# Score blocks on four 32-column tiles of TensorE, and one product with w per chunk in a delta-rule scan

## The chip, the cores and the metric

The kernel runs on one core of a Trainium2 chip. A core has five engines with an instruction stream each: TensorE (PE; its weight loads, PEld, are shown apart), VectorE (DVE), ScalarE (ACT), GpSimd (POOL) and SyncE (SP, which issues DMAs). The metric is the time of one execution on the device, in microseconds (us); less is better.

## The reference, cut to what matters

The program computes two blocks of a network on 1024 tokens of width 1024. The first block holds a mixer with four gated heads and one with twelve. The second holds a hybrid mixer, one branch of which is a delta-rule scan (gdn), on the latent tokens (1024) and before that on a context of 256 tokens. The two pieces that the change touches are these.

```
def _chunk_gated_scan(q, k, v, log_g):        # CHUNK = 32 keys; both directions are needed
    ...
    s = jnp.einsum('bnthk,bnshk->bnhts', q * jnp.exp(b - ref), k * jnp.exp(ref - b))
    s = jnp.where(np.tril(np.ones((CHUNK, CHUNK), bool)), s, 0.0)
    o_intra = jnp.einsum('bnhts,bnshv->bnthv', s, v)
    ...

def gdn_chunked(q, k, v, g, beta, s0):        # chunks of 64 tokens
    ...
    u = jnp.einsum('bnhij,bnhjv->bnhiv', tm, vc * bc[..., None])
    w = jnp.einsum('bnhij,bnhjk->bnhik', tm, kb * jnp.exp(gc)[..., None])
    attn = jnp.einsum('bnhik,bnhjk->bnhij', qc, kc) * decay
    qg = qc * jnp.exp(gc)[..., None]
    kend = kc * jnp.exp(gc[..., -1:] - gc)[..., None]
    def step(s, inp):
        v_new = u_i - jnp.einsum('bhlk,bhkv->bhlv', w_i, s)
        o_i = jnp.einsum('bhlk,bhkv->bhlv', qg_i, s) + jnp.einsum('bhij,bhjv->bhiv', a_i, v_new)
        s = s * ge_i[..., None, None] + jnp.einsum('bhlk,bhlv->bhkv', ke_i, v_new)
        return s, o_i
```

The kernel does not step through `v_new`: for every chunk it forms the products of w with `kend` (here `ke`) and with `attn` (here the "row" or `at`), so that a step of the scan is one small matrix product with the state.

## The kernel before, in words

**Order of the program.** Nobody writes out the order of the instructions: the framework (`schedule_with_timeline_sim=True`) orders each engine's stream when the kernel is built, by the data each instruction needs, by the buffers of the tile pools and by priorities (`g.up()` raises one). On the chip each engine then takes its stream in that order.

**Gated heads (`Gated.unit`).** A head has 128 key features on the partitions and 1024 tokens. It is cut into units of n = 256 tokens, for each of two directions d; so there are (4 + 12) heads x 4 x 2 = 128 units. In a unit, VectorE and ScalarE make scaled copies of q and k: `u_qt`/`u_kt` (scaled within 32 tokens), `u_qa`/`u_kb` (across neighbouring groups of 32), `u_qh`/`u_kh` (across halves of 64). GpSimd makes `u_qh` (L239) and `u_qd` (L241). Then come the score products, for each of the ng = 2 blocks of 128 tokens, all in fp32 with K = 128: one 128x128 product of `u_kt` and `u_qt` (L247), and over parts of its result two 32x32 products of `u_kb` and `u_qa` (L249, L250, or L253, L254) and one 64x64 product of `u_kh` and `u_qh` (L251 or L255). The result goes from PSUM to `A` by ScalarE (d = 1) or by a masked copy on VectorE (d = 0, L261). Each fp32 product appears in the trace as two records of LDWEIGHTS and MATMUL. Between the score products the scheduler puts the projections of the next heads (L139 to L141), the state updates `o<-V,u_kdT` (L225), the transposes `a<-ident,u_kd` (L214) and the outputs (L276 to L280). The first four heads run with the adaLN table in the background (L957 to L975), the twelve others with the context path of the second block.

**The scan (`gdn_scan`).** On the latent tokens it runs for three pairs of heads, and `prepare` for two directions of each: six times in all. `hTb` and `hwb` are wide buffers that hold one direction. In `prepare`, `huw` is made on GpSimd and VectorE and multiplied with `hTb` (L1607); this gives u (in `huw`) and w (in `hwb`). GpSimd makes `ke` (L1616) and the base of `A` (L1619). Then TensorE makes for eight chunk pairs and two heads w times `ke` (L1624, 128 stationary columns and 64 moving) and `ke` times u (L1632, 64x64), which give `A` and `B`. After these, a row of decays comes by DMA, passes ScalarE, VectorE, two `affine_select` on GpSimd (L1651), ScalarE, and is multiplied with `kq` on GpSimd (L1654); TensorE then makes w times this row (L1658, 64 moving) and the row times u (L1667, 64x64), which give `Q` and `O`. `carry` is the chain over 16 chunks (L1696, L1698). On the context (`fin` is given) only `A` and `B` are made. During the first latent pairs another branch (ssd, L1250 to L1346) runs beside the scan. Behind the scan comes the output projection (`MixersOut.group`), whose weights pass through the buffers `mraw`.

Of the kernel before, what the change touches and what calls it, by code (L numbers as in the profile page):

```python
# [10 lines left out]
F32 = mybir.dt.float32  # L11
# [143 lines left out]
class Gated:  # L155
# [14 lines left out]
    def unit(self, d, u, q, k, lg):  # L170
# [71 lines left out]

        ap = g.psum("a")
        for i in range(ng):
            o = i * P
            w = lambda a, lo, hi: a[:, o + lo:o + hi]
            nc.tensor.matmul(ap[:, o:o + P], w(kt, 0, P), w(qt, 0, P), start=True, stop=True)  # L247
            if d == 0:
                nc.tensor.matmul(ap[0:32, o + 32:o + 64], w(kb, 0, 32), w(qa, 32, 64), start=True, stop=True)  # L249
                nc.tensor.matmul(ap[64:96, o + 96:o + 128], w(kb, 64, 96), w(qa, 96, 128), start=True, stop=True)  # L250
                nc.tensor.matmul(ap[0:64, o + 64:o + 128], w(kh, 0, 64), w(qh, 64, 128), start=True, stop=True)  # L251
            else:
                nc.tensor.matmul(ap[32:64, o:o + 32], w(kb, 32, 64), w(qa, 0, 32), start=True, stop=True)  # L253
                nc.tensor.matmul(ap[96:128, o + 64:o + 96], w(kb, 96, 128), w(qa, 64, 96), start=True, stop=True)  # L254
                nc.tensor.matmul(ap[64:128, o:o + 64], w(kh, 64, 128), w(qh, 0, 64), start=True, stop=True)  # L255
# [1272 lines left out]
def gdn_scan(g, pool, wide, n, fm_out, rows, inv, hp, s0, fin=None):  # L1528
# [53 lines left out]
    def prepare(d):  # L1582
# [4 lines left out]
        f = pool.tile([P, 3, ncp, 2], F32, name="hf", tag="hf", bufs=2)  # L1587
# [27 lines left out]
        ke = t4("hke")  # L1615
        nc.gpsimd.tensor_tensor(ke, kt, bc(f[:, 0]), op=ALU.mult)  # L1616

        A = t4("hA", two)
        nc.gpsimd.tensor_tensor(A, g.ident2[:, None, None, :].to_broadcast([P, ncp, 2, 64]), bc(f[:, 2]), op=ALU.mult)  # L1619
        for q0, mm in step4:  # L1620
            ps = bank()
            for i in range(mm * 2):
                cp, h = q0 + i // 2, i % 2
                nc.tensor.matmul(ps[:, i * 64:i * 64 + 64], wb[:, cp * 2 + h], ke[:, cp, h], start=True, stop=True)  # L1624
            As = flat(A[:, q0:q0 + mm])
            with g.up():
                nc.vector.tensor_sub(As, As, ps[:, :mm * P])
            ps = bank()
            for i in range(mm * 2):
                cp, h = q0 + i // 2, i % 2  # L1630
                for e in range(2):
                    nc.tensor.matmul(ps[half[1 - e], i * 64:i * 64 + 64], ke[half[e], cp, h], u(e, cp, h),  # L1632
                                     start=True, stop=True)
# [7 lines left out]
        if fin is not None:  # L1641
            return A, None
        row = gdn_rows(g, pool, n, rows, hp, d, 0, "hx", 2)
        Q = big("hQ", [2, ncp, 64], 4)
        nc.scalar.activation(Q, row, AF.Exp)
        nc.vector.tensor_mul(Q, Q, qE)
        nc.vector.tensor_sub(row, row, hc(col))
        r3 = row.rearrange("p h c i -> p (h c) i")
        s = 1 if d == 0 else -1
        for e in range(2):  # L1650
            nc.gpsimd.affine_select(r3[half[e]], r3[half[e]], pattern=[[0, m], [s, 64]], compare_op=ALU.is_ge,  # L1651
                                    fill=NEG, base=0, channel_multiplier=-s)
        nc.scalar.activation(row, row, AF.Exp)
        nc.gpsimd.tensor_tensor(row, row, kq, op=ALU.mult)  # L1654
        for h in range(2):
            ps = bank()
            for cp in range(ncp):
                nc.tensor.matmul(ps[:, cp * 64:cp * 64 + 64], wb[:, cp * 2 + h], row[:, h, cp], start=True, stop=True)  # L1658
            Qh = Q[:, h].rearrange("p c i -> p (c i)")
            with g.up():  # L1660
                nc.vector.tensor_sub(Qh, Qh, ps[:, :ncp * 64])
        for q0, mm in step4:
            ps = bank()
            for i in range(mm * 2):
                cp, h = q0 + i // 2, i % 2
                for e in range(2):
                    nc.tensor.matmul(ps[half[e], i * 64:i * 64 + 64], row[half[e], h, cp], u(e, cp, h), start=True, stop=True)  # L1667
            Os = flat(O[:, q0:q0 + mm])
            with g.up():
                if d == 0:  # L1670
                    nc.scalar.copy(Os, ps[:, :mm * P])
                else:
                    nc.vector.tensor_add(Os, Os, ps[:, :mm * P])
        return A, Q
# [189 lines left out]
class MixersOut:  # L1864
# [14 lines left out]
    def group(self, gi, finish=None, pool=None):  # L1879
# [570 lines left out]
```

## Time and profile before

| what | value |
|---|---|
| median of 3 runs | 3707.62 us (3703.4 to 3709.96) |
| the profiled execution: its own time | 3706.74 us |
| the profiled execution: span of the core | 3704.5 us |
| PE busy | 3335.8 us (90%) |
| DVE busy | 2592.7 us (70%) |
| ACT, POOL busy | 1600.5 us (43%), 1445.3 us (39%) |

The profile is of one execution, and its time is 0.9 us below the median. Matmuls are pipelined: a record of one lasts longer than the time that the array gives to it, so what a product costs is read from the distance between the starts of records. "Idle before" is an engine's idle time ahead of an instruction, and behind the arrow stands what ended it.

### The profile page before, as it was taken

What the parts mean: (1) busy time and instruction counts of PE and PEld (TensorE: products, weight loads), DVE (VectorE), ACT (ScalarE), POOL (GpSimd) and SP (SyncE); (2) the same over time, 40 slices, a digit from 0 to 9 for tenths busy, and PEclk for the clock granted to TensorE, in tenths of its full rate; (3) what the DMA queues carried; (4) which work ended last, traced back from release to release, by engine and by line L of the source; (5) the groups of instructions that cost most, each with busy time, mean ns of one, the idle gap of its engine ahead of it and who ended that gap; (6) DMA issues with size and microseconds to landing.
All of it is one profiled execution on the core that took longest, in us unless ns stands there. A gap on an engine that the chain in (4) does not pass through costs nothing.

```text
span 3704.5 us, 59873 instructions
## 1 busy us (share of the span) xinstructions
PE 3335.8 (90%) x21896; PEld 2717.0 (73%) x21896; DVE 2592.7 (70%) x5580; ACT 1600.5 (43%) x3332; POOL 1445.3 (39%) x1431
## 2 busy tenths in 40 slices
PE   7998998999979999999999999688996889748887
PEld 6886786766758888879798977566775877536665
DVE  4776664346685767976767685679995555578887
ACT  3343333544424545445545441354433331225565
POOL 4556673000041334333334331723215562335544
PEclk9998999999999999999999999788996879869999
DMA  5223244252352212111112234234337555678994
GB/s 179 78 83 95 86 134 136 79 184 88 91 170 66 70 63 57 51 56 46 46 49 65 64 135 154 76 90 130 113 117 175 119 150 177 212 210 291 302 331 161
DMA packets 373986, 461.04 MB, mean 124 GB/s; under 512 B 150419, under 2 KB 280723, under 8 KB 373692
## 3 DMA queue, kind: packets, MB, share of 16 engines
q1 hardware_dynamic: 359852, 407.93, 35.3%
q0 software_dynamic: 13840, 49.29, 4.4%
q8 instruction: 173, 2.83, 0.3%
q14 instruction: 121, 0.99, 0.1%
HBM read 357.57 MB, written 104.27 MB: 125 GB/s over the span
## 4 chain that ended last, share of the span: by engine, by line
PE 60%; DVE 16%; issue 8%; DMA 7%; POOL 4%; ACT 3%; SPq 1%; DVEq 0%; POOLq 0%; ACTq 0%
PE mm L139 12%; PE mm L140 12%; PE mm L141 11%; PE a L247 2%; DVE elo L2019 2%; PE o L225 1%; DVE cacc L1141 1%; PE a L402 1%; PE a L141 1%; PE a L140 1%; PE f L1099 1%; PE o L276 1%; POOL aw L962 1%; PE a L139 1%; PE a L251 1%
## 5 line engine op out<-in xcount | busy, mean ns | idle before, releaser
L116 POOL TENSOR_TENSOR wlo<-wraw,whi 128x1024 fp32r<-128x1024 f32 (+1 forms) x131 | 328.2, 2510 | 518.3 <-ACT whi L115 496.0
L2017 ACT CAST ehi<-eraw 128x1024 fp32r<-128x1024 f32 x192 | 200.5, 1050 | 147.2 <-PE a L141 101.8
L139 PE MATMUL mm<-x1h,whi 128*128 128x512 f32 x576 | 237.4, 412 | 7.6 <-DVE q L621 3.8
L140 PE MATMUL mm<-x1l,whi 128*128 128x512 f32 x576 | 234.9, 408 | 3.0 <-DVE x1l L133 3.0
L141 PE MATMUL mm<-x1h,wlo 128*128 128x512 f32 x576 | 234.7, 407 | 0.0
L139 PE MATMUL mm<-whi,x1h 128*128 128x256 f32 x768 | 222.4, 290 | 0.0
L2019 DVE TENSOR_TENSOR elo<-eraw,ehi 128x1024 fp32r<-128x1024 f32 x138 | 198.2, 1470 | 32.6 <-ACT ehi L2017 32.4
L141 PE MATMUL mm<-whi,x1l 128*128 128x256 f32 x768 | 219.9, 287 | 0.0
L140 PE MATMUL mm<-wlo,x1h 128*128 128x256 f32 x768 | 219.9, 287 | 0.0
L115 ACT CAST whi<-wraw 128x1024 fp32r<-128x1024 f32 (+1 forms) x131 | 136.0, 1040 | 165.1 <-PE mm L140 90.4
L2021 POOL TENSOR_TENSOR elo<-eraw,ehi 128x1024 fp32r<-128x1024 f32 x54 | 139.6, 2591 | 158.1 <-ACT ehi L2017 135.3
L139 PE MATMUL mm<-whi,xh 128*128 128x256 f32 x640 | 184.9, 289 | 0.0
L140 PE MATMUL mm<-wlo,xh 128*128 128x256 f32 x640 | 183.9, 288 | 0.5 <-POOL wlo L116 0.5
L141 PE MATMUL mm<-whi,xl 128*128 128x256 f32 x640 | 183.4, 287 | 0.0
L139 PE MATMUL mm<-x2h,whi 128*128 128x512 f32 x400 | 166.4, 416 | 6.5 <-ACT cu L1130 3.5
L139 PE MATMUL mm<-whi,yin 128*128 128x512 f32 x352 | 148.6, 425 | 22.3 <-DVE z L820 13.9
L140 PE MATMUL mm<-x2l,whi 128*128 128x512 f32 x400 | 164.7, 412 | 0.0
L141 PE MATMUL mm<-x2h,wlo 128*128 128x512 f32 x400 | 163.8, 410 | 0.8 <-POOL wlo L116 0.8
L139 PE MATMUL mm<-xh,whi 128*128 128x512 f32 x336 | 138.9, 413 | 19.8 <-ACT whi L115 16.6
L239 POOL TENSOR_TENSOR u_qh<-u_qa,facX 128x256 f32<-128x256 f32 x64 | 71.4, 1115 | 202.1 <-DVE u_qa L236 170.9
L139 PEld LDWEIGHTS mm<-whi,x1h 128*128 128x128 f32 x768 | 146.9, 191 | 1.1
L962 POOL TENSOR_SCALAR aw<-aw,ac 128x128 f32<-128x128 f32 x256 | 116.3, 470 | 80.2 <-DMA aw<-in_ada_w_dram 32.5
(755 smaller groups left out, 10700.9 us busy)
## 6 DMA issues: line engine op xcount, KB each, us to landing
eraw<-in_we_gate_dram SPq DMA_DIRECT2D x64, 512.0 KB
eraw<-in_we_up_dram SPq DMA_DIRECT2D x64, 512.0 KB
eraw<-in_we_down_dram SPq DMA_DIRECT2D x64, 512.0 KB
yin<-yd POOLq DMA_DIRECT2D x29, 1024.0 KB, 8.5
aw<-in_ada_w_dram SPq DMA_DIRECT2D x96, 256.0 KB
yd<-y_hl SPq DMA_DIRECT2D x80, 256.0 KB
wraw<-in_w_dram SPq DMA_DIRECT2D x25, 512.0 KB
wraw<-in_w_out_dram SPq DMA_DIRECT2D x24, 512.0 KB
```

Source lines behind the costliest of these rows:

```text
L115: nc.scalar.copy(hi[:, :sz], raw[:, :sz])
L116: nc.gpsimd.tensor_tensor(lo[:, :sz], raw[:, :sz], hi[:, :sz].bitcast(F32), op=ALU.subtract)
L139: nc.tensor.matmul(ps, sh, mh, start=first and i == 0, stop=False)
L140: nc.tensor.matmul(ps, sh, ml, start=False, stop=False)
L141: nc.tensor.matmul(ps, sl, mh, start=False, stop=last and i == n - 1)
L225: nc.tensor.matmul(up[:, :Vd], kdT[:, i * P:(i + 1) * P], V[:, gi, :], start=True, stop=True)
L239: nc.gpsimd.tensor_tensor(v3(qh, 32), v3(qa, 32), bcast(fqh, nck, 32), op=ALU.mult)
L247: nc.tensor.matmul(ap[:, o:o + P], w(kt, 0, P), w(qt, 0, P), start=True, stop=True)
L962: nc.gpsimd.tensor_scalar(w[:, k], w[:, k], at(k), 0.0, op0=ALU.mult, op1=ALU.add)
L2017: nc.scalar.copy(hi, raw)
L2019: nc.vector.tensor_sub(lo, raw, hi.bitcast(F32))
L2021: nc.gpsimd.tensor_tensor(lo, raw, hi.bitcast(F32), op=ALU.subtract)
```

## The change

In the gated heads every score product now writes 32 keys, on one of the four 32-column tiles of TensorE (`c` = 0 to 3), and only the queries that are used: 32, 64, 128 and 128 of them for `u_kt`/`u_qt` (in the other direction 128, 128, 64, 32), 32 for the two products of `u_kb`/`u_qa`, and 64 for two products of `u_kh`/`u_qh`, which stand behind those of both blocks. In the scan, `ke` and the row share one buffer `kr` (128 columns for a chunk and head), so that one product with w gives both; for this the row is made ahead of the products with w, the products with u are issued together, and `po` is a second PSUM bank. Three buffers change: `kr` has twice the size of `ke`, `hf` has one buffer in place of two, and `mraw` has two in place of three.

```diff
+        def block(i, c, sta, mov, lo, hi):
+            o = i * P
+            nc.tensor.matmul(ap[32 * c:32 * c + 32, o + lo:o + hi], sta[:, o + 32 * c:o + 32 * c + 32], mov[:, o + lo:o + hi],
+                             start=True, stop=True)
+        within = ((0, 32), (0, 64), (0, P), (0, P)) if d == 0 else ((0, P), (0, P), (64, P), (96, P))
         for i in range(ng):
-            o = i * P
-            w = lambda a, lo, hi: a[:, o + lo:o + hi]
-            nc.tensor.matmul(ap[:, o:o + P], w(kt, 0, P), w(qt, 0, P), start=True, stop=True)
-            if d == 0:
-                nc.tensor.matmul(ap[0:32, o + 32:o + 64], w(kb, 0, 32), w(qa, 32, 64), start=True, stop=True)
-                nc.tensor.matmul(ap[64:96, o + 96:o + 128], w(kb, 64, 96), w(qa, 96, 128), start=True, stop=True)
-                nc.tensor.matmul(ap[0:64, o + 64:o + 128], w(kh, 0, 64), w(qh, 64, 128), start=True, stop=True)
...
+            for c in range(4):
+                block(i, c, kt, qt, *within[c])
+            for c in (d, d + 2):
+                block(i, c, kb, qa, *((32 * c + 32, 32 * c + 64) if d == 0 else (32 * c - 32, 32 * c)))
+        for i in range(ng):
+            for c in (2 * d, 2 * d + 1):
+                block(i, c, kh, qh, 64 - 64 * d, P - 64 * d)
...
-        f = pool.tile([P, 3, ncp, 2], F32, name="hf", tag="hf", bufs=2)
+        f = pool.tile([P, 3, ncp, 2], F32, name="hf", tag="hf", bufs=1)
...
-        ke = t4("hke")
+        kinds = 1 if fin is not None else 2
+        kr = big("hke", [ncp, 2, kinds, 64])
+        ke = kr[:, :, :, 0]
         nc.gpsimd.tensor_tensor(ke, kt, bc(f[:, 0]), op=ALU.mult)
+        if fin is None:
+            row = gdn_rows(g, pool, n, rows, hp, d, 0, "hx", 2)
...
+            at = kr[:, :, :, 1]
+            nc.gpsimd.tensor_tensor(at.rearrange("p c h i -> p h c i"), row, kq, op=ALU.mult)
...
+        per = 4 // kinds
+        for q0 in range(0, ncp, per):
...
+                nc.tensor.matmul(ps[:, i * wd:(i + 1) * wd], wb[:, cp * 2 + h], kr[:, cp, h], start=True, stop=True)
...
+                nc.vector.tensor_sub(A[:, q0:q0 + mm], A[:, q0:q0 + mm], p5[:, :, :, 0])
+                if fin is None:
+                    Qs = Q[:, :, q0:q0 + mm].rearrange("p h c i -> p c h i")
+                    nc.vector.tensor_sub(Qs, Qs, p5[:, :, :, 1])
...
                 for e in range(2):
-                    nc.tensor.matmul(ps[half[1 - e], i * 64:i * 64 + 64], ke[half[e], cp, h], u(e, cp, h),
-                                     start=True, stop=True)
+                    nc.tensor.matmul(ps[half[1 - e], io], ke[half[e], cp, h], u(e, cp, h), start=True, stop=True)
+                if fin is None:
+                    for e in range(2):
+                        nc.tensor.matmul(po[half[e], io], at[half[e], cp, h], u(e, cp, h), start=True, stop=True)
...
-                raw = zp.tile([P, 512], F32, name="mraw", tag="mraw", bufs=max(nb, 2))
+                raw = zp.tile([P, 512], F32, name="mraw", tag="mraw", bufs=2)
```

The change also moves instructions, since the scheduler orders the new program anew. On PE, in a forward unit of one of the twelve heads, this stood before (names are result, moving and stationary operand; the shape is that of the result):

```order
L140 MATMUL mm<-x1l,whi 128x512
L247 MATMUL a<-u_qt,u_kt 128x128
L249 MATMUL a<-u_qa,u_kb 32x32
L250 MATMUL a<-u_qa,u_kb 32x32
L251 MATMUL a<-u_qh,u_kh 64x64
...
L141 MATMUL mm<-x1h,wlo 128x512
```

In the changed kernel a forward unit of those heads reads as follows; the four columns of products of the second block repeat those of the first and are left out:

```order
L139 MATMUL mm<-x1h,whi 128x512
L249 MATMUL a<-u_qt,u_kt 32x32
L249 MATMUL a<-u_qt,u_kt 32x64
L225 MATMUL o<-V,u_kdT 128x128 x2
L249 MATMUL a<-u_qt,u_kt 32x128 x2
L249 MATMUL a<-u_qa,u_kb 32x32 x2
...
L249 MATMUL a<-u_qh,u_kh 32x64 x4
L214 MATMUL a<-ident,u_kd 128x128 x2
```

Sixteen small products stand in place of eight, and in this unit a state update of the full width (L225) comes between them. Over the whole program the score products stand in 199 unbroken stretches before and in 257 now, for 128 units; 42 units are unbroken now, and 69 were.

On PE, in the first direction of the first pair of the latent scan, the products with w and with u stood so before:

```order
L1624 MATMUL tr<-hke,hwb 128x64 x8
L1632 MATMUL o<-huw,hke 64x64 x16
...
L1658 MATMUL tr<-hx,hwb 128x64 x8
L1658 MATMUL o<-hx,hwb 128x64 x8
L1667 MATMUL tr<-huw,hx 64x64 x16
L1667 MATMUL o<-huw,hx 64x64 x16
```

Now they stand so:

```order
L1649 MATMUL tr<-hke,hwb 128x128 x4
L1649 MATMUL o<-hke,hwb 128x128 x4
...
L1663 MATMUL tr<-huw,hke 64x64 x16
...
L1666 MATMUL o<-huw,hke 64x64 x16
L1663 MATMUL tr<-huw,hke 64x64 x2
L1666 MATMUL o<-huw,hke 64x64 x2
```

There are 16 products with w for a direction where there were 32, each with 128 moving columns; the products of `ke` with u and of the row with u, which were apart, alternate for the second half.

On POOL, in the same place, `ke` (L1616, now L1624) and the row (L1654, now L1638) stood so before:

```order
L1599 TENSOR_TENSOR huw<-hv,rtgl 128x8x64 x2
...
L1651 AFFINE_SELECT hx<-hx 64x1024 x2
...
L1654 TENSOR_TENSOR hx<-hx,hkq 128x1024
L1616 TENSOR_TENSOR hke<-hk,hf 128x1024
```

and now:

```order
L1624 TENSOR_TENSOR hke<-hk,hf 128x16x64
L1603 TENSOR_TENSOR huw<-hv,rtgl 128x8x64 x2
L1641 TENSOR_TENSOR hA<-ident_102,hf 128x1024
L1634 AFFINE_SELECT hx<-hx 64x1024 x2
...
L1638 TENSOR_TENSOR hke<-hx,hkq 128x2x8x64
```

The last row of the first of these two fences is the `ke` of the second direction, made while TensorE still used the row; in the second fence both halves of the buffer `hke` are made ahead of the products with w.

## Rows read from the trace of the kernel before

**Rows 1.** The page, its head and the busy time of each engine.
```profile
span 3704.5 us, 59873 instructions
PE 3335.8 (90%) x21896; PEld 2717.0 (73%) x21896; DVE 2592.7 (70%) x5580; ACT 1600.5 (43%) x3332; POOL 1445.3 (39%) x1431
```

**Rows 2.** Windows: stretch, its length, busy us (records) of each engine, granted clock, DMA.
```profile
core 0: us, PE busy (x) PEld busy (x) DVE busy (x) ACT busy (x) POOL busy (x), PEclk, DMA share, GB/s
70.00:600.00 530.00, 506.45 (x3289) 427.16 (x3288) 366.68 (x955) 204.49 (x470) 334.09 (x507) 0.97 0.31 95
...
1150.00:1380.00 230.00, 229.87 (x1531) 203.79 (x1530) 160.61 (x460) 114.22 (x286) 72.89 (x65) 1.00 0.21 67
...
1380.00:2240.00 860.00, 840.09 (x5983) 719.46 (x5982) 644.23 (x1826) 429.87 (x1089) 316.30 (x343) 0.99 0.20 64
1460.00:1540.00 80.00, 77.16 (x539) 65.17 (x539) 75.41 (x236) 43.86 (x115) 33.30 (x43) 0.98 0.19 55
...
2830.00:3080.00 250.00, 214.53 (x2345) 196.58 (x2347) 146.16 (x227) 88.04 (x181) 141.71 (x120) 0.81 0.61 160
```

**Rows 3.** The page, chain of work that ended last, by engine.
```profile
PE 60%; DVE 16%; issue 8%; DMA 7%; POOL 4%; ACT 3%; SPq 1%; DVEq 0%; POOLq 0%; ACTq 0%
```

**Rows 4.** PE timeline, one forward unit: start us, us from first start to last end.
```profile
1507.46 0.38 PE L247 MATMUL a<-u_qt,u_kt 128*128 128x128 f32 x2
1507.77 0.22 PE L249 MATMUL a<-u_qa,u_kb 128*32 128x32 f32 x1
1507.78 0.22 PE L250 MATMUL a<-u_qa,u_kb 128*32 128x32 f32 x1
1507.82 0.20 PE L249 MATMUL a<-u_qa,u_kb 128*32 128x32 f32 x1
...
1507.95 0.33 PE L251 MATMUL a<-u_qh,u_kh 128*64 128x64 f32 x2
1508.21 0.49 PE L247 MATMUL a<-u_qt,u_kt 128*128 128x128 f32 x2
1508.63 0.22 PE L249 MATMUL a<-u_qa,u_kb 128*32 128x32 f32 x1
...
1508.82 0.33 PE L251 MATMUL a<-u_qh,u_kh 128*64 128x64 f32 x2
1509.08 0.50 PE L139 MATMUL mm<-x1h,whi 128*128 128x512 f32 x1
1509.41 0.40 PE L140 MATMUL mm<-x1l,whi 128*128 128x512 f32 x1
1509.65 0.39 PE L141 MATMUL mm<-x1h,wlo 128*128 128x512 f32 x1
```

**Rows 5.** PE timeline: column tiles in the attention, and 32x32 products on one tile.
```profile
649.60 0.39 PE L458 MATMUL o<-pT,v 128*64 128x128 f32 x4
649.82 0.39 PE L463 MATMUL o<-pT,v 128*64 128x128 f32 x4
...
2772.89 1.19 PE L1510 MATMUL a<-gys,gH 32*32 32x32 f32 x32
```

**Rows 6.** PE timeline of the latent scan: two rows of its first direction.
```profile
2861.95 1.15 PE L1667 MATMUL tr<-huw,hx 64*64 64x64 f32 x32
2862.93 1.10 PE L1667 MATMUL o<-huw,hx 64*64 64x64 f32 x32
```

**Rows 7.** Groups by line, 2840 to 3082 us: count, then busy us and mean ns.
```profile
L1624 PE MATMUL tr<-hke,hwb 128*128 128x64 f32 x192 | 33.8, 343 | 7.7 <-DVE hwb L1613 7.7
...
L1632 PE MATMUL o<-huw,hke 64*64 64x64 f32 x384 | 20.2, 265 | 0.0
...
L1658 PE MATMUL tr<-hx,hwb 128*128 128x64 f32 x96 | 16.4, 337 | 0.0
...
L1654 POOL TENSOR_TENSOR hx<-hx,hkq 128x1024 f32<-128x1024 f32 x6 | 14.1, 2356 | 0.4 <-ACT hx L1653 0.2
...
L1658 PE MATMUL o<-hx,hwb 128*128 128x64 f32 x96 | 14.1, 302 | 0.0
```

**Rows 8.** L1616 on POOL (ns: least, median, longest), and what `mraw` waited for.
```profile
L1616 POOL TENSOR_TENSOR hke<-hk,hf x12: 609/1308/2407, 2048.2 to 3051.0; 128x256 f32<-128x256 f32 x6, 128x1024 f32<-128x1024 f32 x6
...
  DMA mraw<-in_w_out_dram: 3.4, 5
```

More of the change, by code (lines that the diff above doesn't have):

```diff
@@ L1614, in prepare @@
         u = lambda e, cp, h: uw[cp // nh][half[e], cp % nh, h, 0:64]
-        ke = t4("hke")
+        kinds = 1 if fin is not None else 2
+        kr = big("hke", [ncp, 2, kinds, 64])
+        ke = kr[:, :, :, 0]
         nc.gpsimd.tensor_tensor(ke, kt, bc(f[:, 0]), op=ALU.mult)
+        if fin is None:
+            row = gdn_rows(g, pool, n, rows, hp, d, 0, "hx", 2)
+            Q = big("hQ", [2, ncp, 64], 4)
+            nc.scalar.activation(Q, row, AF.Exp)
+            nc.vector.tensor_mul(Q, Q, qE)
+            nc.vector.tensor_sub(row, row, hc(col))
+            r3 = row.rearrange("p h c i -> p (h c) i")
+            s = 1 if d == 0 else -1
+            for e in range(2):
+                nc.gpsimd.affine_select(r3[half[e]], r3[half[e]], pattern=[[0, m], [s, 64]], compare_op=ALU.is_ge,
+                                        fill=NEG, base=0, channel_multiplier=-s)
+            nc.scalar.activation(row, row, AF.Exp)
+            at = kr[:, :, :, 1]
+            nc.gpsimd.tensor_tensor(at.rearrange("p c h i -> p h c i"), row, kq, op=ALU.mult)
@@ L1618, in prepare @@
         A = t4("hA", two)
         nc.gpsimd.tensor_tensor(A, g.ident2[:, None, None, :].to_broadcast([P, ncp, 2, 64]), bc(f[:, 2]), op=ALU.mult)
+        per = 4 // kinds
+        for q0 in range(0, ncp, per):
+            mm = min(per, ncp - q0)
+            ps = bank()
+            wd = kinds * 64
+            for i in range(mm * 2):
+                cp, h = q0 + i // 2, i % 2
+                nc.tensor.matmul(ps[:, i * wd:(i + 1) * wd], wb[:, cp * 2 + h], kr[:, cp, h], start=True, stop=True)
+            p5 = ps[:, :mm * 2 * wd].rearrange("p (c h x i) -> p c h x i", h=2, x=kinds, i=64)
+            with g.up():
+                nc.vector.tensor_sub(A[:, q0:q0 + mm], A[:, q0:q0 + mm], p5[:, :, :, 0])
+                if fin is None:
+                    Qs = Q[:, :, q0:q0 + mm].rearrange("p h c i -> p c h i")
+                    nc.vector.tensor_sub(Qs, Qs, p5[:, :, :, 1])
@@ L1620, in prepare @@
         for q0, mm in step4:
             ps = bank()
+            po = bank() if fin is None else None
             for i in range(mm * 2):
                 cp, h = q0 + i // 2, i % 2
[L1624 to L1630, printed above, removed]
+                io = slice(i * 64, i * 64 + 64)
@@ L1631, in prepare @@
                 for e in range(2):
-                    nc.tensor.matmul(ps[half[1 - e], i * 64:i * 64 + 64], ke[half[e], cp, h], u(e, cp, h),
-                                     start=True, stop=True)
+                    nc.tensor.matmul(ps[half[1 - e], io], ke[half[e], cp, h], u(e, cp, h), start=True, stop=True)
+                if fin is None:
+                    for e in range(2):
+                        nc.tensor.matmul(po[half[e], io], at[half[e], cp, h], u(e, cp, h), start=True, stop=True)
@@ L1640, in prepare @@
                                    ps[half[1 - e], :mm * P].rearrange("p (c i) -> p c i", i=P))
[L1641 to L1674, printed above, removed]
+                if fin is None:
+                    Os = flat(O[:, q0:q0 + mm])
+                    if d == 0:
+                        nc.scalar.copy(Os, po[:, :mm * P])
+                    else:
+                        nc.vector.tensor_add(Os, Os, po[:, :mm * P])
+        return (A, None) if fin is not None else (A, Q)
     B = big("hB", [m, 2, 64], 1 if fin is not None else 2)
```

4 lines of the change are left out of this document (removed).

## The prediction

> **What bounds the kernel now.** The page's head and its busy times come first [rows 1]: PE is busy for 90% of the span and DVE for 70%, with ACT and POOL far behind. An average hides stages, so the windows come next [rows 2]. In the gated heads, where half of the change lies, PE is the bound: 229.87 of 230 us, then 840.09 of 860 us, and 506.45 of 530 us for the first four heads. DVE has 644.23 us of work in the 860, so it has room on average, but in some 80 us stretches it has 75.41 us, with almost none. In the scan PE is busy for 214.53 of 250 us, at a granted clock of 0.81 and not 0.97 to 1.00. The chain that ended last [rows 3] says the same: 60% of it is PE, 16% DVE. Time taken from PE's stream in the gated heads should thus come off the end nearly whole, as long as DVE keeps up.
>
> **A unit's score products before.** The timeline shows starts, and the distance between starts is what a product costs [rows 4]. From L247 to the next product lies 0.31 us: two records of 128 moving columns at 0.11 each (the distance that the attention's records of 128 columns keep on a tile: four of L458, two heads on two column tiles, in 0.22 us [rows 5]) and some 0.10 for the change from a full-width stationary operand to a 32-column one. The two products of 32, side by side, take 0.18 to the next: two records of 0.027, an uncovered load of the same size and again 0.10 for a change of shape; that of 64 takes 0.26 in the same way. The second L247 takes 0.42: its 0.22, a change of shape, and a weight load of 128 columns that nothing covers, 0.10. Then 0.19 and 0.26 follow. All of it is 1509.08 − 1507.46 = 1.62 us. The wide product behind it is 0.33 from its successor and not 0.24, so that another 0.10 goes to its uncovered load. With 128 units and 199 unbroken stretches this makes 128 × 1.62 + 199 × 0.10 = **227 us** of PE.
>
> **A unit after.** All products have one shape, 32 columns, so the changes within a unit go, and only entering and leaving a stretch remain. Entering costs 0.10 for the change and about 0.03 for an uncovered load of 32 columns (an estimate: a quarter of the 0.10 for 128). Leaving costs 0.10 and 0.10 as above. The new order has 257 stretches, as other work now comes between the products of 86 units: 257 × 0.33 = **85 us**.
>
> The rest is the stream of the products. Before, no row has four 32-column tiles at work. The nearest are the attention's two 64-column tiles, which stream side by side without costing each other anything [rows 5]; and L249 and L250 on different tiles start 0.01 apart [rows 4]. So a record of 128 moving columns is taken at 0.11, of 64 at 0.055, of 32 at 0.027, two of each to a product. The fullest tile of a forward unit is the third, with 128 and 32 columns in each of two blocks: 2 × 2 × (0.11 + 0.027) = 0.55 us. That is the lower bound, with four free tiles. If a product must also wait until the one before it in the stream has started, the short ones queue behind the long, and I count 0.69. If only two tiles stream at a time, the 544 columns of a block's products (32 + 64 + 128 + 128 + 32 + 32 + 64 + 64) cost 544 × 2 × 0.86 ns = 0.93 us one behind another, and two blocks two at a time again 0.93. I take 0.65, since rows 4 show starts that do not wait, and order in the stream must hold to some degree. 128 × 0.65 = 83, and with the 85 a unit's score products cost **168 us**. PE gains 227 − 168 = 59. Of it I let 0.8 pass to the end, since PE is busy for 98 to 100% of the large windows but DVE is near its limit in some [rows 2]: **−47**. The bounds are 72 passing whole (body 0.55) and 18 (body 0.93: 204 in place of 168, 23 × 0.8).
>
> DVE, ACT and POOL do the same work per unit. GpSimd's u_qh and DVE's u_kh now have the products of both blocks ahead of them and lose nothing by being late.
>
> **The products with w.** Before, 384 records: L1624 33.8 us, L1658 16.4 and 14.1 [rows 7], 64.3 in all, or 0.167 each, for only 64 moving columns. The cost is the load of 128 stationary columns. Afterwards there are 192 records with 128 moving columns under the same loads: 64.3 / 2 = 32 us less on PE. In the scan PE is busy for 86% [rows 2] and the chain also runs through DVE and POOL, so half of it passes: −16 (bounds −32 and 0).
>
> **The products with u.** They stay 64x64, 384 records of L1632 in 20.2 us [rows 7] and 384 of L1667, of which 32 took 0.98 us [rows 6], 31 ns each, 12 us in all. Where both kinds now alternate they write other halves and could run on more tiles at once: between 0 and −16, half of 32. They alternate for half of the stream in the first direction, so I take −5.
>
> **The wait for GpSimd.** `ke` takes up to 2.41 us [rows 8] and the row 2.36 [rows 7]. The first product with w needed only `ke`; now it needs the row too, with the DMA, ACT, DVE and affine_select steps ahead of it. Behind the waiting product on PE stand the products with u, then carry, and all of pair d waits. If PE had nothing else, both ops would show each time: 6 × (2.41 + 2.36) = 28. With the other direction and ssd's products beside it, I take a third, +9 (bounds 0 and +28). DVE subtracts the same elements in twice as many instructions for `Q` and `A`, which I count at nothing, since it has 146.16 us of work in the 250 [rows 2]; uncovered, these would add to the upper bound, not to the sum.
>
> **Buffers.** `hf` in one buffer makes the second direction wait for the last reader of the first, and `mraw`, whose DMA waited 3.4 us in 5 places [rows 8] with three buffers, has two. I take +3 for both, bounds 0 and +10. The scan and its surroundings: −16 − 5 + 9 + 3 = **−9**, with bounds at −32 and +10.
>
> **Sum.** −47 − 9 = −56. The profiled execution's own time is 3706.7, which gives **3651**; the median is 0.9 above it, which changes nothing.
>
> **Rivals.**
> *Two tiles at a time, or a fixed distance between starts* (0.18). The only long train of short products here, 32 records of 32x32, takes 1.19 us to its last end, less than 0.2 of which is that end's, some 31 ns a record [rows 5]; the 64x64 ones take 31 ns too [rows 6]. For 32 records in a unit this is 0.93 to 1.0, as with two tiles. PE then gains some 20, the whole is −18 to −16 with −9 for the scan: about 3681. Against it: two starts 0.01 apart [rows 4].
>
> *A smaller fixed distance* (0.06). With 25 ns a record a unit needs 32 × 0.025 = 0.80, the sum is 187, 40 × 0.8 = 32 passes, and −32 − 9 ends at 3666. Such a floor is what the Trainium skill states ("TensorE: Matmul & The Clock Gate", section "Wait — 56ns, not 53.3ns?"): start to start never drops below about 25 ns however small the product. The trace neither confirms nor denies it for different tiles: starts 0.01 apart stand in each unit, but only in twos, and no long train goes below 30 ns.
>
> *DVE takes over in the gated heads* (0.12). Only a third of 59 passes, 20, and with −9 for the scan 3678. For it: 75.41 of 80 us [rows 2]. Against it: 644.23 of 860.
>
> *Slower: four tiles that run one after another* (0.06). If products on different column tiles of one shape do not run side by side, a unit's stream is 2 × 0.93 = 1.87 us, in all 239 + 85 = 324 against 227: +97, with −9 for the scan 3795. The change loses once the stream of a unit exceeds (227 − 85) / 128 = 1.11 us. For it: before, each product has one tile and no row shows four. Against it: the attention's 4 records in 0.22 us [rows 5].
>
> *More than forecast* (0.03): body 0.55, all passing, and −32 from the scan, 3603.
>
> **How the numbers follow.** My forecast (3620 to 3680 around 3651) has 0.55, the others the chances above. The range goes from 3603 (−72 − 32) to 3700 (−18 and +10, at the edge of the second rival), which leaves out the slow rival and mishaps above it. A measurement of this kernel can tell about 0.2%, 7 us, from no change. Faster by more than that is the forecast and the first three rivals, less 0.06 for those that end with DVE and a wait on GpSimd together: 0.88. The same is 0.03, slower 0.09: the slow rival and half of the rest.
>
> **What the changed profile would show.** An unbroken unit's score products lie within about 0.9 us, first start to the next wide product, where they took 1.62; records on the four tiles start within about 0.01 of each other. PE's busy time in the gated heads falls by some 45 to 60 us, DVE's share of the same stretches rises by a few points, and the twelve heads end some 35 us sooner. The 192 records of products with w stand as far apart as before with twice the moving columns. In the scan, PE waits for GpSimd's row ahead of the first product with w. I am wrong on the main step if records of one unit follow each other at 30 ns or more with the tiles changing, if PE's idle time grows behind DVE by what its busy time loses, or if entering and leaving a stretch costs much more than 0.33. I am wrong on the scan if its stretch does not shorten.

## The result, and the profile after

The changed kernel takes 3648.7 us (median of 4 runs, 3641.68 to 3659.12) against 3705.59 us for the kernel before on the same chip: a ratio of 0.9847, 95% interval 0.9821 to 0.9874. That is 57 us less, where 56 were forecast. The profiled execution has a span of 3656.9 us, 47.6 below the profiled one of before; it is the slowest of its four runs, so that 47.6 is what the traces can explain.

The page's head, busy times and chain by engine, after (they answer to [rows 1, 3]):

```profile
span 3656.9 us, 63623 instructions
PE 3228.8 (88%) x23752; PEld 2610.4 (71%) x23752; DVE 2576.0 (70%) x5604; ACT 1595.0 (44%) x3332; POOL 1439.0 (39%) x1431
...
PE 46%; DVE 23%; DMA 9%; issue 9%; POOL 8%; ACT 3%; SPq 2%; DVEq 0%; POOLq 0%; ACTq 0%
```

PE lost 107 us of busy time and the span 48. PE's share of the chain went from 60 to 46%, DVE's from 16 to 23%. The windows of [rows 2], after:

```profile
core 0: us, PE busy (x) PEld busy (x) DVE busy (x) ACT busy (x) POOL busy (x), PEclk, DMA share, GB/s
70.00:600.00 530.00, 496.60 (x3876) 421.79 (x3874) 361.54 (x962) 208.19 (x483) 347.14 (x515) 0.98 0.32 98
1150.00:1380.00 230.00, 220.83 (x1750) 191.50 (x1749) 151.85 (x431) 108.86 (x273) 65.58 (x60) 0.98 0.20 64
1380.00:2240.00 860.00, 822.53 (x7292) 691.57 (x7291) 655.57 (x1845) 427.84 (x1093) 307.96 (x349) 0.99 0.22 70
...
2830.00:3080.00 250.00, 195.37 (x2291) 167.03 (x2289) 161.10 (x277) 81.39 (x170) 136.12 (x117) 0.84 0.60 154
```

In the 230 us where PE had almost no gap (0.13 us) it now has 9. One whole, unbroken unit on PE's timeline, after (answers to [rows 4]; the last column's xN counts records, and there are 32):

```profile
1487.04 0.31 PE L249 MATMUL a<-u_qt,u_kt 128*32 128x128 f32 x6
1487.14 0.20 PE L249 MATMUL a<-u_qa,u_kb 128*32 128x32 f32 x1
1487.17 0.27 PE L249 MATMUL a<-u_qt,u_kt 128*32 128x128 f32 x1
...
1487.48 0.30 PE L249 MATMUL a<-u_qh,u_kh 128*32 128x64 f32 x4
1487.57 0.19 PE L249 MATMUL a<-u_qa,u_kb 128*32 128x32 f32 x1
...
1487.62 0.22 PE L249 MATMUL a<-u_qh,u_kh 128*32 128x64 f32 x1
1487.76 0.50 PE L140 MATMUL mm<-x1l,whi 128*128 128x512 f32 x1
1488.10 0.40 PE L141 MATMUL mm<-x1h,wlo 128*128 128x512 f32 x1
```

The first start and the last are 0.58 us apart, the next wide product starts 0.14 later, and it is again 0.34 from its successor. In place of 1.62 us stands 0.72. So the arithmetic of an unbroken unit held. What PE then waits for between the first unit and the last, after:

```profile
engine line waited for: us in total, times, longest us
PE a L214 <- DVE u_kd L210: 27.1, 21, 4.7
PE tr L314 <- DVE s_y L291: 9.1, 9, 2.6
PE mm L139 <- DVE z L824: 8.5, 6, 2.7
```

and the first of these rows in the same stretch of the kernel before:

```profile
PE a L214 <- DVE u_kd L210: 6.0, 5, 2.7
```

The transposes of `u_kd`, which open a unit, wait for VectorE 21 us longer. Part of what PE gave up has become waiting.

For a place where the time came from, I read three marks in each profiled execution: the start of the last output product of the gated heads (`o<-V,A`), that of the last product `a<-gys,gH`, which is just ahead of the latent scan, and the span.

| | heads end | between | `gys` to the end | span |
|---|---|---|---|---|
| before | 2242.6 | 558.3 | 903.6 | 3704.5 |
| after | 2217.4 | 556.9 | 882.6 | 3656.9 |
| difference | −25.2 | −1.4 | −21.0 | −47.6 |

The forecast was right in its sum, but not in its parts: −47 was to come from the heads and −9 from the scan. In the scan the groups of products stand so, after (they answer to [rows 7]):

```profile
L1663 PE MATMUL tr<-huw,hke 64*64 64x64 f32 x384 | 20.3, 236 | 3.3 <-DVE hQ L1655 3.3
L1666 PE MATMUL o<-huw,hke 64*64 64x64 f32 x384 | 19.7, 243 | 3.9 <-DVE hQ L1655 3.9
L1649 PE MATMUL tr<-hke,hwb 128*128 128x128 f32 x96 | 17.4, 337 | 13.2 <-POOL hke L1638 8.5 <-DVE hwb L1617 4.7
...
L1649 PE MATMUL o<-hke,hwb 128*128 128x128 f32 x96 | 15.6, 311 | 0.0
```

The products with w take 33.0 us where they took 64.3, with twice the moving columns in each. Ahead of them PE now waits for GpSimd's row, 8.5 us.

### The profile page after: what moved, and what is told of

Same layout as the page of the kernel before. It is cut to its first block, busy times and chain, and to the rows that moved or that the text cites. A ratio compares the mean times of both kernels' runs of the same rounds, so it can differ in the third digit from the quotient of the medians.

```text
span 3656.9 us, 63623 instructions
## 1 busy us (share of the span) xinstructions
PE 3228.8 (88%) x23752; PEld 2610.4 (71%) x23752; DVE 2576.0 (70%) x5604; ACT 1595.0 (44%) x3332; POOL 1439.0 (39%) x1431
## 4 chain that ended last, share of the span: by engine, by line
PE 46%; DVE 23%; DMA 9%; issue 9%; POOL 8%; ACT 3%; SPq 2%; DVEq 0%; POOLq 0%; ACTq 0%
PE mm L139 9%; PE mm L140 9%; PE mm L141 9%; PE a L249 2%; POOL aw L966 2%; DVE cacc L1145 2%; DVE elo L2025 2%; DMA srow<-rdsl 1%; DMA aw<-in_ada_w_dram 1%; PE a L406 1%; PE o L225 1%; POOL wlo L116 1%; DVE gtmp L1465 1%; PE a L141 1%; DVE u_kb L187 1%
## 5 line engine op out<-in xcount | busy, mean ns | idle before, releaser
L115 ACT CAST whi<-wraw 128x1024 fp32r<-128x1024 f32 (+1 forms) x131 | 136.0, 1040 | 158.0 <-PE mm L140 78.5
L139 PE MATMUL mm<-whi,yin 128*128 128x512 f32 x352 | 150.2, 430 | 23.4 <-DVE z L824 14.1
L966 POOL TENSOR_SCALAR aw<-aw,ac 128x128 f32<-128x128 f32 x256 | 123.7, 498 | 85.5 <-DMA aw<-in_ada_w_dram 51.9
L140 PEld LDWEIGHTS mm<-wlo,x1h 128*128 128x128 f32 x768 | 146.8, 191 | 0.6
```

Of the source, the lines that this page charges most:

```text
L115: nc.scalar.copy(hi[:, :sz], raw[:, :sz])
L139: nc.tensor.matmul(ps, sh, mh, start=first and i == 0, stop=False)
L140: nc.tensor.matmul(ps, sh, ml, start=False, stop=False)
L966: nc.gpsimd.tensor_scalar(w[:, k], w[:, k], at(k), 0.0, op0=ALU.mult, op1=ALU.add)
```

## The experiments

Each kernel was compared with the kernel before on its own chip; "ratio" is to that. The marks of all of them, from one profiled execution each:

| | heads end | between | `gys` to the end | span | median of the runs |
|---|---|---|---|---|---|
| e1 score blocks alone | 2211.9 | 570.6 | 888.2 | 3670.7 | 3674.6 |
| e2 scan alone | 2246.6 | 564.4 | 889.1 | 3700.1 | 3700.4 |
| e3 buffers alone | 2248.1 | 560.7 | 928.1 | 3736.9 | 3724.8 |
| e4 no cross products | 2158.6 | 561.7 | 902.2 | 3622.5 | 3622.1 |
| e5 tile by tile | 2239.7 | 562.5 | 900.7 | 3702.9 | 3698.3 |
| e6 w apart | 2215.8 | 556.8 | 912.3 | 3684.9 | 3698.9 |
| e7 u apart | 2216.2 | 560.2 | 875.2 | 3651.6 | 3653.1 |
| e8 score blocks and buffers | 2208.6 | 556.8 | 895.4 | 3660.8 | 3667.4 |
| e9 without u_kt's product | 2182.2 | 561.1 | 896.6 | 3639.9 | 3645.6 |
| e10 raised priority | 2189.3 | 553.7 | 889.1 | 3632.1 | 3626.3 |
| e11 old buffers, hQ in three | 2211.3 | 570.7 | 883.9 | 3665.9 | 3669.9 |
| e12 e10, u_kt on GpSimd | 2174.4 | 562.5 | 900.6 | 3637.5 | 3639.3 |

The middle stretch has no edited instruction, and it still runs from 553.7 to 570.7: with each edit the scheduler orders the whole program anew. The last stretch moves as much: the changed kernel, e5, e9, e10 and e12 have the same code there and need 882.6 to 900.7. One kernel's difference in a stretch is therefore uncertain by 10 to 20 us, and I compare means where several kernels share an edit.

**e1, the score blocks alone.** The edit is the first hunk of the diff.

> The kernel before with the score blocks alone; the scan and the buffers stay. Theory (read from the two traces): the gated heads end about 25 us sooner, since of some 60 us that PE gains there half turns into waits for DVE's u_kd, and the scan's part of the gain is the scan's own; 3706 - 25 = 3681 (3671 to 3690). Rival, the prediction's terms as they stand: 47 of the 56 come from the score blocks, 3659. Second rival: the new order around the scan, not its products, gave the scan's gain, so that this kernel has it too: about 3657.

Ratio 0.9923 (0.9906 to 0.9939), 28.7 us less than before on its chip. The heads end 31 us sooner. The first theory holds for the heads, and the prediction's −47 does not. The other marks move too, though nothing was edited there: the middle is 12 us longer and the last stretch 15 shorter. So a shorter last stretch alone does not show that the scan's change works.

**e2, the scan and its buffers alone.** The edit is the other hunks.

> The kernel before with the scan's change and its buffers alone; the score blocks stay. Theory: the scan gives some 24 us, most of it from the 192 records of products with w that are left out (32 us of PE): 3682 (3672 to 3691). Rival, the prediction's terms: -9, 3697. Second rival: the gain came from the order and shows in neither half alone: within 4 us of before.

Ratio 0.9994 (0.9979 to 1.001): nothing that can be told from no change. By the marks the last stretch is 14.5 us shorter, as it was in e1 with the old scan, but the heads end 4 later and the middle is 6 longer, with no line of either edited. The theory's 24 was too much, and the prediction's −9 lies just outside the interval; the second rival, within 4 us of before, is met by the time. The two halves measured alone (28.7 + 3) do not add up to 57.

**e3, the buffers alone.**

```diff
-        f = pool.tile([P, 3, ncp, 2], F32, name="hf", tag="hf", bufs=2)
+        f = pool.tile([P, 3, ncp, 2], F32, name="hf", tag="hf", bufs=1)
...
-                raw = zp.tile([P, 512], F32, name="mraw", tag="mraw", bufs=max(nb, 2))
+                raw = zp.tile([P, 512], F32, name="mraw", tag="mraw", bufs=2)
```

> The kernel before with hf in one buffer and mraw in two, nothing else. Prediction: +3 (0 to +10), 3709. Rival: mraw's two buffers cost more, since the trace after shows DVE waiting 6.6 us for its DMA and the chain that ended last running through it: +6 to +10, 3714. Rival: nothing at all, within 2 us.

Ratio 1.0061 (1.0039 to 1.0083): 21 us slower, more than any theory gave. What VectorE waits for from the `gys` products on, in e3:

```profile
engine line waited for: us in total, times, longest us
DVE srow L1301 <- DMA srow<-rdsl: 56.4, 13, 7.5
...
DVE mraw L1890 <- DMA mraw<-in_w_out_dram: 12.9, 9, 4.2
```

and the same row before:

```profile
DVE srow L1301 <- DMA srow<-rdsl: 23.9, 12, 4.2
```

The wait for `mraw` grew by 9.5 us over its 3.4 [rows 8], but that for `srow` by 32, and no buffer of `srow` was touched: it belongs to the branch beside the scan.

**e4, a larger gain on PE.** Before, with the `u_kb`/`u_qa` and `u_kh`/`u_qh` products left out.

```diff
             nc.tensor.matmul(ap[:, o:o + P], w(kt, 0, P), w(qt, 0, P), start=True, stop=True)
-            if d == 0:
...
-                nc.tensor.matmul(ap[64:128, o:o + 64], w(kh, 64, 128), w(qh, 0, 64), start=True, stop=True)
```

> The kernel before without the products of u_kb/u_qa and u_kh/u_qh (left out of the computation); one 128x128 product per block is left. A unit's score products take 0.44 in place of 1.62 us, and no shape changes are left: PE loses about 128 x 1.18 = 151 us of work in the gated heads, two and a half times what the score blocks save. Theory, that DVE and its waits hold what PE gives up: the heads end 50 to 70 us sooner, a share well under a half, 3645 (3630 to 3660). Rival, the prediction's 0.8 of PE's gain: 120 us sooner, 3586.

Ratio 0.9775 (0.9754 to 0.9797), 81 us less. The heads end 84 us sooner, of some 160 that PE was spared: about half. That is more than the theory gave and far less than 0.8 (but see below: the half is a mean over stages that differ).

**e5, the same products, one tile after the other.**

```diff
-        for i in range(ng):
-            for c in range(4):
-                block(i, c, kt, qt, *within[c])
...
+        for c in range(4):
+            for i in range(ng):
+                block(i, c, kt, qt, *within[c])
+                if c in (d, d + 2):
+                    block(i, c, kb, qa, ...)
+                if c in (2 * d, 2 * d + 1):
+                    block(i, c, kh, qh, ...)
```

> The changed kernel with a unit's score products in another order: all of the first column tile, then all of the second, and so on. Same products, shapes and sizes. Theory: TensorE takes its stream in order and holds only a few products for a tile, so that tiles run side by side only where the stream alternates between them; a unit's stream goes from 0.58 to 1.3 to 1.9 us, 90 to 170 us more PE work over 128 units, half of which reaches the end: 3705 (3690 to 3735). Rival: each tile has a queue as deep as it needs, the order doesn't matter, 3650.

Ratio 0.9978 (0.9963 to 0.9994): nearly the whole gain of the changed kernel is gone. One unit on PE's timeline, e5:

```profile
1427.43 0.25 PE L249 MATMUL a<-u_qt,u_kt 128*32 128x32 f32 x2
1427.51 0.23 PE L249 MATMUL a<-u_qa,u_kb 128*32 128x32 f32 x2
1427.57 0.28 PE L249 MATMUL a<-u_qh,u_kh 128*32 128x64 f32 x2
1427.69 0.23 PE L249 MATMUL a<-u_qt,u_kt 128*32 128x32 f32 x2
...
1428.67 0.27 PE L249 MATMUL a<-u_qt,u_kt 128*32 128x128 f32 x1
1428.87 0.50 PE L140 MATMUL mm<-x1l,whi 128*128 128x512 f32 x1
```

The first tile's records now follow each other one by one, and the unit takes 1.44 us (1.17 in the other direction) with the same products that took 0.72. So here tiles ran side by side only so far as the stream alternated between them; the time, 3698.3, lies in the theory's range.

**e6, two products with w again.** The row stays ahead of them.

```diff
-                nc.tensor.matmul(ps[:, i * wd:(i + 1) * wd], wb[:, cp * 2 + h], kr[:, cp, h], start=True, stop=True)
+                for x in range(kinds):
+                    nc.tensor.matmul(ps[:, i * wd + x * 64:i * wd + x * 64 + 64], wb[:, cp * 2 + h], kr[:, cp, h, x],
+                                     start=True, stop=True)
```

> The changed kernel with two products with w per chunk and head again, one for ke and one for the row, one behind the other; all else stays. PE gets back 192 records at the same distance as now, some 30 us of work in the scan. Prediction: half of it shows, 3664 (3658 to 3670). Rival: all shows, since the products stand in the way of the chain, 3679. Rival: none, because the scan waits for DMA and DVE of the branch beside it: 3649.

Ratio 0.9985 (0.9969 to 1.0002): 50 us more than the changed kernel by the medians; 30 in the last stretch of the profile, which is of the fastest of its twelve runs. The groups in e6:

```profile
L1650 PE MATMUL o<-hke,hwb 128*128 128x64 f32 x192 | 38.8, 369 | 12.0 <-DVE hwb L1617 12.0
L1650 PE MATMUL tr<-hke,hwb 128*128 128x64 f32 x192 | 38.0, 366 | 8.9 <-DVE hwb L1617 8.7
```

192 + 192 records of half the columns cost 76.8 us, where 96 + 96 cost 33.0: 44 us, not the 30 expected, and more than the 64.3 of the kernel before. Two thirds of it show in the profile and all of it by the medians, above each of the three forecasts. Not all of the 50 need be the products: the granted clock of e6's twelve runs is 0.925 to 0.931, where the changed kernel's four have 0.935 to 0.937, and no run separates the two.

**e7, the products with u apart.**

```diff
                 for e in range(2):
                     nc.tensor.matmul(ps[half[1 - e], io], ke[half[e], cp, h], u(e, cp, h), start=True, stop=True)
-                if fin is None:
-                    for e in range(2):
+            for i in range(mm * 2 if fin is None else 0):
...
+                for e in range(2):
                         nc.tensor.matmul(po[half[e], io], at[half[e], cp, h], u(e, cp, h), start=True, stop=True)
```

> The changed kernel with the products of ke with u and those of the row with u apart, all of the one kind before the other for four chunk pairs. In the trace alternating records stand 15 ns apart and those of one kind 30 ns; undone, PE gets about 768 x 0.5 x 15 ns = 6 us more. Prediction (a term of -5 for the alternation): 3654 (3649 to 3660). Rival: nothing on the path, 3649 within 4.

Ratio 0.9865 (0.984 to 0.9889), 4 us more than the changed kernel, and 7 less in the last stretch: inside the scatter. The prediction's −5 is neither confirmed nor denied by the time. The alternation itself is plain in the changed kernel's timeline:

```profile
2818.20 1.15 PE L1663 MATMUL tr<-huw,hke 64*64 64x64 f32 x32
...
2880.96 0.23 PE L1663 MATMUL tr<-huw,hke 64*64 64x64 f32 x2
2880.97 0.23 PE L1666 MATMUL o<-huw,hke 64*64 64x64 f32 x2
2881.01 0.23 PE L1663 MATMUL tr<-huw,hke 64*64 64x64 f32 x2
2881.03 0.22 PE L1666 MATMUL o<-huw,hke 64*64 64x64 f32 x2
2881.07 0.23 PE L1663 MATMUL tr<-huw,hke 64*64 64x64 f32 x2
```

Where one kind stands alone, 32 records take 1.15 us to the last end, 30 ns from start to start. Where both alternate, four records start within 0.055 us, about 15 ns each: half.

**e8, the score blocks with the buffers.** e1 and the edits of e3.

> The kernel before with the score blocks, hf in one buffer and mraw in two; the scan's products as before. The score blocks alone came to 3674.6, the buffers alone cost 21. Theory: the buffers cost what they cost before, since mraw's weights arrive one buffer later for the output projection: 3695 (3688 to 3702), and the scan's products then give 45 in the changed kernel. Rival: the 21 belong to the order that the scheduler came to in that kernel, and here the buffers cost the +3 of the prediction: 3678.

Ratio 0.9904 (0.9881 to 0.9927), 37 us less than before and 7 less than e1. Here the buffers cost nothing in sum, so the 21 us of e3 are not what two buffers cost in any kernel; the rival was nearer. In the profiles the middle stretch is 14 us shorter than in e1, and the last one, where `mraw` is used, is 7 longer.

**e9, less work for VectorE.** The changed kernel without one multiplication.

```diff
-        nc.vector.tensor_mul(kt, kt, k)
```

> The changed kernel without the multiplication of u_kt by k on DVE (left out of the computation): 128 instructions of 0.41 us, 53 us of DVE in the gated heads, 40 of them in the twelve. Theory: about half of what PE gains in the heads is lost to waits for DVE (19 us for u_kd alone in the twelve heads), so that work taken from DVE gives it back: heads end 15 to 25 us sooner, 3630 (3620 to 3640). Rival: PE waits for the length of a unit's chain over several engines or for the order, not for DVE's amount of work: within 6 us of the changed kernel.

The heads end 35 us sooner than in the changed kernel (31 by the mean of the kernels with the score blocks), more than the theory asked for, and PE's wait for `u_kd` went from 27.1 to 18.6:

```profile
PE a L214 <- DVE u_kd L210: 18.6, 13, 6.8
```

The whole is at 0.9854 (0.9839 to 0.9869), about the changed kernel's ratio: the last stretch, where nothing was edited, is 14 us longer in the profile. My number for the whole was wrong, the one for the heads right in kind.

**e10, raised priority for the score products.** The changed kernel with the two loops over `block` under `g.up()`.

```diff
+        with g.up():
             for i in range(ng):
...
```

> The changed kernel with a unit's score products at raised priority, so that fewer other products come between them: 145 stretches in place of 257. By the prediction's 0.33 us for entering and leaving a stretch, PE gets 112 x 0.33 = 37 us less work; with the half that passed so far, 3630 (3622 to 3640). Rival: products put ahead of others hold up the transposes and state updates that DVE and ACT wait for, and nothing is gained: 3649 or slower.

Ratio 0.9798 (0.9783 to 0.9813), 3626.3 us: the fastest of the kernels that compute the whole result (e4 leaves products out). The heads end 28 us sooner than in the changed kernel, where a half of 37 would be 18. It is not a gain everywhere. The last `o<-V,A` of the first four heads starts at 615.7 us, 16 later than the mean of the kernels with the score blocks (599.4), and the twelve heads more than make it up. What PE waits for most in e10's heads:

```profile
PE f L979 <- POOL aacc L973: 20.9, 9, 5.0
```

In the changed kernel that wait is 5.8 us. So the theory fits the twelve heads and the rival, products ahead of others, the first four.

**e11, the old buffers.** `hf` in two, `mraw` in three, and `hQ` in three in place of four.

> The changed kernel with hf in two and mraw in three buffers as before; hQ gives up one of its four buffers for the room. In the changed kernel DVE waits 7 us for mraw's transfers and the output projection gives back some 15 us of what the scan gained. Theory: the buffers bring a part of that, 3640 (3633 to 3646). Rival, as with the score blocks, where these two buffers cost nothing: 3649 within 6. Rival: the third buffer of hQ holds up the next pair, 3655 to 3665.

Ratio 0.9916 (0.9902 to 0.9929), some 21 us above the changed kernel. In the marks, which hold 9 of it, the middle stretch is 14 longer, and none of these buffers is in use there, while the last stretch is 1 longer; so this run shows the scatter rather than a cost of `hQ`, and the question of the buffers stays open.

**e12, e10 with that multiplication on GpSimd.**

```diff
-        nc.vector.tensor_mul(kt, kt, k)
+        nc.gpsimd.tensor_tensor(kt, kt, k, op=ALU.mult)
```

> The kernel of e10_up with the multiplication of u_kt by k on GpSimd in place of DVE. GpSimd has about 350 us free in the twelve heads' 1130 us beyond what it waits through; one such op takes it 0.9 to 1.0 us by u_qh's rows. Theory (the kernel without that multiplication ended the heads 37 us sooner): DVE's 53 us less bring part of that in the heads, 10 to 30 us there, and 3610 (3596 to 3630) at the end, with some 15 us to either side by what the order does to the scan. Rival: u_kt comes later from the slower engine and holds up the score products: the heads end no sooner or later than in e10_up, 3626 to 3645.

Ratio 0.9826 (0.9807 to 0.9844), slower than e10 by 13 us by the medians and by 10 by the ratios; 3639.3 lies outside the expected 3596 to 3630. The heads end 15 us sooner than in e10, in the expected 10 to 30, but the middle and the last stretch are 9 and 12 longer. The 15 us come from the first four heads alone, which end at 595.3 us and not at 615.7; the twelve take 5 us longer than in e10. So this run does not show that the twelve heads gain by less work for VectorE, and the kernel as a whole did not.

## Why the prediction was right, and where it was not

**The unit: right.** From starts of records, with every distance cut at 0.45 us so that waits stay out, all score products took 210.5 us before and 136.0 after. With 0.10 for the wide load behind each stretch (202 and 268 in the traces) this makes 231 and 163; forecast were 227 and 168. A unit's stream took 0.58, between the 0.55 of four free tiles and the 0.65 taken. PE was spared 68 us, forecast 59.

**Tiles and fixed distances.** The rival of two tiles at a time (0.93) and that of tiles in series (1.87) fell on the 0.58; e5 shows that the second was no idle one, since the order of the products in the stream decides. The rival of 25 ns for each record also fell: 32 records in 0.58 us are 18 ns each, and within a unit records on different tiles start 0.01 and less apart. The Trainium skill ("TensorE: Matmul & The Clock Gate", section "Wait — 56ns, not 53.3ns?") gives that distance as a floor from start to start, however small the product; the trace does not agree for products on different tiles, while e5's records of 32 columns on one tile, some 0.03 apart, do not go below it.

**What passes to the end: the step that failed.** I let 0.8 of PE's gain pass, "since PE is busy for 98 to 100% of the large windows". Over all heads the runs give a half, at four sizes of the gain. The stream is reckoned as in the first point, the heads' end is the mark; "score blocks" is the mean of the six kernels with the score blocks and no other edit in the heads (2213.5), the three without have a mean of 2245.8. The two columns on the right take it apart at the start of the last `o<-V,A` of the first four heads (615.5 without, 599.4 with score blocks).

| step | score stream on PE | heads end | first four: stream, end | twelve: stream, rest of the heads' end |
|---|---|---|---|---|
| without to with score blocks | 231 to 163: −68 | −32 (0.47) | −20, −16 (0.8) | −48, −16 (0.33) |
| score blocks to e5 | 163 to 224: +61 | +26 (0.43) | +18, +12 (0.7) | +43, +14 (0.31) |
| score blocks to e10 | 163 to 118: −45 | −24 (0.53) | −2, +16 | −43, −41 (0.94) |
| without to e4 | 231 to 70: −161 | −87 (0.54) | −42, −20 (0.49) | −119, −67 (0.56) |

In this run the −47 was thus −25 (−19 in the first four heads, −7 in the rest), and −32 as a mean. The half is no constant but a mean of two stages. In the first four heads, in whose window PE was busy for 96% (506.45 of 530 us), the forecast's 0.8 held for the score blocks; in the twelve, where it was busy for 98 to 100%, a third passed, 16 us where "some 35" were forecast. The busy share thus did not tell what PE's gain is worth. The rival "a third passes, VectorE takes over" (0.12) describes the twelve heads, and the four do not follow it.

What became of the rest in the twelve heads is idle time of PE, 20 us before and 46 after, with the same work on VectorE (806 us); before, then after, in the columns of [rows 2]:

```profile
1149.40:2242.80 1093.40, 1073.36 (x7528) 926.15 (x7528) 806.14 (x2290) 545.41 (x1379) 390.07 (x410) 0.99 0.21 65
1134.00:2217.50 1083.50, 1037.44 (x9063) 881.37 (x9063) 806.67 (x2290) 542.01 (x1379) 376.82 (x410) 0.99 0.21 65
```

The largest part of it is the wait for `u_kd` (6.0 to 27.1 us in all heads). Distances above 0.45 us behind a score product's record add up to 3 us before and 27 after (the full sums are 213.4 and 163.5); 24 of the 27 lie behind the last product of a stretch, and 10 of them are that same wait for `u_kd`. e9 shows the other side: taking 53 us from VectorE, which looked as if it had room (655.57 of 860), brought the heads' end 31 us ahead of that mean, 0.59 of the work. It is one kernel, but 31 is well above the 9 us by which the six differ, so VectorE's work is on the path as PE's is. Why a PE busy for 98% of a window is not the bound for 98% of its time is my reading and no run tests it alone: a short wait is followed by a backlog that hides it in the share. Waits are not all of it either: the granted clock over the heads is 0.96 in e4 and e10 where before has 0.97.

**The products with w: right in PE time.** 64.3 to 33.0 us; −32 was forecast. "Half of it passes" is less sure: e6 gives back 44 us of PE time and is 30 slower by the profile, 50 by the medians.

**The products with u.** On PE the distance is halved where the kinds alternate. Over the whole latent scan, from start to start with the cut at 0.45 us, they take 34.3 us before, 23.4 after and 27.9 in e7: −11, between the −5 taken and the far bound of −16. In time it cannot be seen (e7).

**The wait for GpSimd.** Forecast +9; the trace has 8.5 us of it, in 2 waits, of which one is 8.4. That they agree is partly luck: the other kernels with this scan have 0 (e6) to 13.8 us (e7). The distances above 0.45 us in PE's stream between the first product with w and the last of `carry` add up to 29.5 us before and 52.9 after, so that PE's other waits, for `hB` and `srow` above all, grew too.

**Scan and buffers: mis-sized.** From `gys` to the end the five kernels with the scan as before need 888 to 928 us, 903.5 in the mean; the eight with the changed scan 875 to 901, 889.7 in the mean. The scan gives about 14, with a scatter of the same size, against 9; in the changed kernel's profile it gave 21. Without e3, which alone has 928, the 14 is 8, and e1 with the old scan needs 888.2: that the scan's change brings any of it is not shown beyond the scatter. The +3 for the buffers could not be settled: +21 in e3, −7 in e8. The bounds given for the scan, −32 and +10, are also not those of its terms, which add up to −48 and +38; and the 0.88 for faster holds only with the 0.03 of "more than forecast", which its sentence leaves out.

So the sum came out by luck: a term that was 22 too large stood beside one that was 12 too small, and the medians lie 9 us further apart than the two profiled executions. What stays open is why the two halves alone give 32 us less and together 57. By the marks the middle stretch, which neither edits, accounts for 20 of it (12 and 6 us longer than before in e1 and e2, 1 shorter in the changed kernel), and in e1 the unedited last stretch is 15 shorter. I put this down to the order that the scheduler finds; no run here held the order fixed, so that is not shown.

## What to carry to other kernels

Small products of one column-tile shape run side by side if the stream alternates between the tiles: write the loop over tiles innermost, and try priority for such a group so that nothing of full width comes between; here that gained in the twelve heads and lost in the first four. Before a gain on a busy engine is taken to the end, look for the next engine's share of the chain, and read what passes from each stage by itself: a half over all heads was 0.8 in one stage and a third in the other. When a scheduler orders the program, an edit moves stretches that it does not touch by 10 us or more, so read stage marks of several kernels before a difference of that size is given a cause.

## What the hardware showed that I had not expected

Records on different 32-column tiles started 6 to 7 ns apart at the head of a unit, and a unit's 32 records 18 ns on average, where in e5 the same records on one tile need some 30 ns (32 moving columns) to 107 (128). Two kinds of 64x64 products that write different halves went from 30 to 15 ns a record by alternating alone. A record of a product with w with 128 moving columns cost hardly more PE time than one with 64: 33.0 us for 192 records after, and 64.3 us for 384 before, 0.17 us each.
